# Linear attention's levels: keys and queries decayed by one product, with one exponential, and each head's scores from its own 64 partitions

## The chip, the cores and the metric

The kernel runs on one core of a Trainium2 chip. Its metric is the time of one execution on the device in microseconds, the median of several runs; lower is better.

## The reference, cut to what matters

One step of a hybrid decoder: a prompt of 2048 tokens and 64 sample tokens (8 sequences of 8) pass a norm, one input projection, two mixers, and one output projection. Mixer A is dilated window attention. Mixer B, which the change concerns, is gated linear attention (GLA) with 4 heads, key width 64 and value width 128:

```python
def step(state, xs):
    qc, kc, vc, gc = xs
    b = jnp.cumsum(gc, axis=2)
    diff = b[:, :, :, None, :] - b[:, :, None, :, :]
    decay = jnp.exp(jnp.where(causal[:, :, None], diff, -jnp.inf))
    scores = jnp.einsum('bhtk,bhsk,bhtsk->bhts', qc, kc, decay)
    o = (jnp.einsum('bhts,bhsv->bhtv', scores, vc)
         + jnp.einsum('bhtk,bhkv->bhtv', qc * jnp.exp(b), state))
    ...
```

`gc` is the log of a data-dependent forget gate. All results are float32.

## The kernel before

The program is one list of Python generators. A function `weave` interleaves the steps of several generators by their expected step counts, and that fixes the order in which instructions are written down. The framework's tile context (`schedule_with_timeline_sim=True`) then puts each engine's instructions into an order of its own, by a model of when each would be ready; every engine runs its list strictly in that order.

The stages are: projections of v, q, k with the window attention, then the projection qkb with the rest of the attention, then the GLA stage (about 820 to 1148 us of the span), then the output stage (1148 us to the end). In the GLA stage the projections g, vb and gb run on TensorE (PE) as the host work (line 1120, 24 float16 matmuls of 512 columns per tile of 128 tokens for vb and gb; g has 24 of 272 and 24 of 256), and GLA is woven between them. The weights of the output projection (w_o, two halves) are fetched and split in the same stage. The output stage combines attention and GLA per token tile (`combine`, lines 1501 to 1545), turns the result on PE (`tm`, line 1453), and multiplies by w_o (`Y`, line 1488: 48 matmuls per tile); the sample tokens' attention is woven between (values, `OS`, line 1737), and their own output `Y_s` comes near the end.

GLA for the prompt handles 256 tokens (two chunks of 128) at a time: eight groups, e0 to e7, after the 64 sample tokens. A group first turns keys, queries and gates to columns (`ptg`, `pg`, `u`), forms the running sum `b` of the log gates, and then gets the scores within a chunk in seven levels, B = 1, 2, 4, ..., 64 (the sample tokens have three). At level B the tokens are cut into pairs of blocks of B; queries of each second block meet keys of the first one, both decayed to the border between the blocks. Per level of a group (`gla_core`, lines 198 to 258):

- POOL writes `D` (lines 207 and 208): border minus `b` for first halves, `b` minus border for second halves, 128x256 each. `D` has two buffers.
- ACT takes the exponentials into `E` by three instructions (line 212): first halves for 128 partitions, and second halves apart for partitions 0 to 63 and 64 to 127, since the two heads of a pair lie on the two halves of the partitions and each gets its own slab of `E`, the other half of which stays zero.
- DVE multiplies keys by `E` into `ks` (line 219, 128x256) and queries by both slabs into `qbd` (line 223, 128x512). `E`, `ks` and `qbd` have two copies, which alternate.
- PE multiplies 64 keys with the queries of both heads at once: 8 float32 matmuls (line 247) of 128 rows, 64 keys and 2x32 queries; the zeros keep the heads apart. A float32 matmul shows as two passes, so 16 in the trace. They go to one PSUM tile of the pool `ps_S`, which has two buffers. At B = 64 there are 4 matmuls of 128 columns (line 232).
- DVE puts the scores into `Ac` where the level's mask says so (`copy_predicated`, line 253, 128x256). At B = 64, ACT copies them to `full` (line 238).

After the levels, `Ac` is copied to `full` (line 264), and for each chunk PE forms the state's update `U` (line 1280), and the output `O` (lines 1288 and 1294); `gla_out` norms it and stores it to `ob_d` (line 303). The DMAs are issued on SP's queue. Memory of the GLA stage is given back after e7's end and used again for the tiles of `combine`, the first of which is loaded as `oc` (line 1505).

Of the kernel before, what the change touches and what calls it, by code (L numbers as in the profile page):

```python
# [18 lines left out]
P = 128  # L19
D = 1024  # L20
# [32 lines left out]
def tile_hymba(ctx: ExitStack, tc: tile.TileContext, A: dict):  # L53
# [80 lines left out]
    def gla_core(pools, st, row0, n, C, levels, scan_m, mask, tagp, full=None):  # L134
# [19 lines left out]
            dd[:C].unsqueeze(2).to_broadcast([C, nch * 4, 64]),  # L154
# [4 lines left out]
        kq = gt.tile([P, 2, 2, n], F32, name=f"kq_{tagp}", tag="kqg", bufs=2)  # L159
        kT, qT = kq[:, 0], kq[:, 1]  # L160
# [37 lines left out]
        for li, B in enumerate(levels):  # L198
            bv = bf.rearrange("p (m two B) -> p m two B", two=2, B=B)
            M = 2 * n // (2 * B)  # L200
            ref = bv[:, :, 0, B - 1 : B].to_broadcast([P, M, B])


            E = st["E"][li % 2]
            D = gt.tile([P, 2, n], F32, name=f"D_{tagp}_{B}", tag="D", bufs=2)
            dv = D[:].rearrange("p a (m B) -> p a m B", B=B)
            POOL.tensor_tensor(dv[:, 1], bv[:, :, 1, :], ref, ALU.subtract)
            POOL.tensor_tensor(dv[:, 0], ref, bv[:, :, 0, :], ALU.subtract)
            for i, (rows, half) in enumerate(
                ((slice(0, P), 0), (slice(0, 64), 1), (slice(64, P), 1))  # L210
            ):
                ACT.activation(E[rows, i, :n], D[rows, half], AF.Exp, scale=1.0 / 16.0)  # L212
            ks, qbd = st["ks"][li % 2], st["qbd"][li % 2]
            kv, qv = (
                f.rearrange("p a c -> p (a c)").rearrange("p (m two B) -> p m two B", two=2, B=B)
                for f in (kT, qT)
            )
            ev = E[:, :, :n].rearrange("p i (m B) -> p i m B", B=B)
            DVE.tensor_tensor(  # L219
                ks[:, : 2 * n].rearrange("p (m two B) -> p m two B", two=2, B=B)[:, :, 0, :],  # L220
                kv[:, :, 0, :], ev[:, 0], ALU.mult,
            )
            DVE.tensor_tensor(
                qbd[:, :, :n].rearrange("p i (m B) -> p i m B", B=B),
                qv[:, :, 1, :].unsqueeze(1).to_broadcast([P, 2, M, B]), ev[:, 1:3], ALU.mult,
            )
            sc = ps_s.tile([P, 512], F32, name=f"sc_{tagp}_{B}", tag="S")
            if B == 64:

                for c in range(nch):  # L230
                    for p in range(2):
                        PE.matmul(
                            sc[:64, (c * 2 + p) * P : (c * 2 + p + 1) * P],
                            ks[:, p * n + c * C : p * n + c * C + 64],
                            qbd[:, :, (p * nch + c) * 64 : (p * nch + c + 1) * 64],
                            start=True, stop=True,
                        )
                ACT.activation(
                    full[0:64, :, 64:], sc[:64].rearrange("p (g t) -> p g t", t=64), AF.Copy
                )  # L240
                yield
                continue
            for c in range(nch):
                for p in range(2):
                    o = (c * 2 + p) * 64
                    for k0 in range(0, C, 64):
                        PE.matmul(
                            sc[k0 : k0 + 64, o : o + 64],
                            ks[:, p * n + c * C + k0 : p * n + c * C + k0 + 64],
                            qbd[:, :, p * (n // 2) + (c * C + k0) // 2 :][:, :, :32],  # L250
                            start=True, stop=True,
                        )
            DVE.copy_predicated(
                Ac[:C].rearrange("p g (m two B) -> p g m two B", two=2, B=B)[:, :, :, 1, :],
                mask[:C, li].bitcast(I32).unsqueeze(1)
                .to_broadcast([C, nch * 4, 32]).rearrange("p g (m B) -> p g m B", B=B),
                sc[:C, : nch * 128].rearrange("p (g m B) -> p g m B", g=nch * 4, B=B),
            )
            yield
# [89 lines left out]
    with ExitStack() as c1:  # L349
# [894 lines left out]
        st = {"wgu": wgu, "E": [], "ks": [], "qbd": []}  # L1244
        for i in range(2):
            for lst, nm_, shape in (
                (st["E"], "E", [P, 3, 256]), (st["ks"], "ks", [P, 512]),
                (st["qbd"], "qbd", [P, 2, 256]), (Sbd, "Sbd", [P, 2, 256]),
            ):
                t = gst.tile(shape, F32, name=f"{nm_}{i}")  # L1250
                POOL.memset(t[:], 0.0)
                lst.append(t)
# [6 lines left out]
        def gla_prompt(e):  # L1259
# [9 lines left out]
            for c in range(2):  # L1269
# [16 lines left out]
                for p in range(2):  # L1286
# [5 lines left out]
                    for j in range(2):  # L1292
                        h = 2 * p + j
                        PE.matmul(
                            O[:, h * P : (h + 1) * P], full[:, c * 4 + h, :],
# [14 lines left out]
        def sample_gla():  # L1310
# [26 lines left out]
            for p in range(2):  # L1337
# [13 lines left out]
                for j in range(2):  # L1351
                    h = 2 * p + j
                    PE.matmul(
                        O[:NS, h * P : (h + 1) * P], Am[:NS, h, :],
                        vb[:NS, h * P : (h + 1) * P], start=False, stop=(j == 1),
                    )
# [531 lines left out]
```

## Time and profile before

| | |
|---|---|
| median of 3 runs | 1423.52 us (1422.46 to 1428.86) |
| the profiled execution | 1426.68 us, of which its span 1424.9 us |
| mean granted TensorE clock | 0.966 |
| busy in the span: PE, DVE, ACT, POOL | 90%, 71%, 59%, 44% |
| GLA stage up to the last `O` (lines 1288, 1294) | to 1108.4 us |
| first `Y` matmul | 1148.2 us |

A profile line names a group of instructions by line, engine, operation and tiles, `out<-in`. PE stands for matmuls, PEld for their weight loads. In the table of windows each engine has its busy time and, in brackets, its number of instructions, and PEclk is the clock that TensorE was granted. A waits line has the total in us, the number of waits and the longest. Matmuls overlap, so a row of n matmuls lasts n pitches and one matmul's fill.

### The profile page before, as it was taken

To read this page: it belongs to the slowest core of one execution; us is meant where nothing else is said; L and a number is where in the kernel's file an instruction comes from. 1 tells how busy PE (TensorE), PEld (TensorE's weight loads), DVE (VectorE), ACT (ScalarE), POOL (GpSimd) and SP (SyncE) were. 2 spreads that over 40 slices of the span, in tenths; PEclk is the share of its full clock that TensorE was granted. 3 is DMA by queue.
4 is the path that set the end of the run, shared out by engine and by line. 5 is a ranking of instruction groups with operands and counts; after the bars stand their busy time and mean duration, and the time that the engine had idled before them with its cause. 6 is when DMAs were issued, how large, how long until landed. Compare 5 with 4: busy or idle time off the path is not lost.

```text
span 1424.9 us, 26506 instructions
## 1 busy us (share of the span) xinstructions
PE 1285.0 (90%) x8942; PEld 743.6 (52%) x8942; DVE 1018.0 (71%) x2459; ACT 843.7 (59%) x2259; POOL 621.9 (44%) x564
## 2 busy tenths in 40 slices
PE   5989999889898898996889999889999989999997
PEld 2434555455455554664667666666555434444343
DVE  6797697789798967666775357898877797773222
ACT  6466787667377775875677665777876542221120
POOL 0144355566577455554421486556551264340000
PEclk9999999999999899997999999999999999999998
DMA  8469756678966797888976444242235759998661
GB/s 297 156 188 255 192 161 150 182 203 215 240 165 173 208 288 239 260 217 228 234 190 179 149 123 116 87 153 91 88 119 176 267 179 344 359 316 267 221 215 63
DMA packets 246874, 283.27 MB, mean 199 GB/s; under 512 B 117889, under 2 KB 148690, under 8 KB 246738
## 3 DMA queue, kind: packets, MB, share of 16 engines
q1 hardware_dynamic: 246738, 281.57, 67.1%
q8 instruction: 71, 1.16, 0.4%
q14 instruction: 65, 0.53, 0.1%
HBM read 183.19 MB, written 75.24 MB: 181 GB/s over the span
## 4 chain that ended last, share of the span: by engine, by line
PE 35%; DVE 25%; DMA 16%; ACT 11%; issue 7%; POOL 4%; SPq 2%; DVEq 0%; POOLq 0%; ACTq 0%
PE Y L1488 7%; PE acc_g L1120 3%; PE acc_vb L1120 3%; PE acc_k L1120 3%; DMA k<-in_cache_k_win 2%; POOL pr L980 2%; PE s L408 2%; PE OS L1737 2%; PE acc_qkb L1120 2%; ACT p L419 2%; DMA o_d<-o 2%; DMA oc<-o_d 2%; DVE p L416 2%; PE acc_v L1120 2%; DMA T_q<-qp_d 2%
## 5 line engine op out<-in xcount | busy, mean ns | idle before, releaser
L980 POOL TENSOR_TENSOR pr<-k,qb 128x512 f32<-128x512 f32 x128 | 171.8, 1342 | 184.9 <-DVE sck L981 113.9
L1120 PEld LDWEIGHTS <-hr 128*128 128x128 f16 x1824 | 177.7, 100 | 138.2 <-issue 17.6
L419 ACT ACTIVATE p<-p,o 128x256 f32<-128x256 f32 (+1 forms) x384 | 173.1, 453 | 86.0 <-DVE o L416 83.3
L1120 PEld LDWEIGHTS <-hl 128*128 128x128 f16 x1248 | 123.2, 100 | 146.6 <-issue 22.2
L1488 PE MATMUL Y<-w_o,mh 128*128 128x512 f16 x768 | 182.9, 385 | 8.3 <-ACT mh L1454 4.9
L416 DVE CUSTOM_DVE_ANT_0 p<-s,m3w,scl_s 128x256 f32<-128x256 f32 (+1 forms) x384 | 143.6, 419 | 39.0 <-DMA o_d<-o 20.3
L393 POOL TENSOR_TENSOR pt<-p,pt 128x512 f16<-128x512 f32 (+1 forms) x80 | 98.3, 1229 | 139.6 <-ACT pt L392 107.3
L441 PE MATMUL O<-v,pt 128*128 128x128 f16 x1200 | 116.1, 224 | 25.3 <-POOL pt L393 10.0
L426 PE MATMUL t<-ident,p 128*128 128x128 f32 x600 | 119.0, 289 | 14.5 <-ACT p L419 9.2
L1488 PEld LDWEIGHTS <-mh 128*128 128x128 f16 x768 | 72.5, 99 | 103.7 <-issue 25.2
L408 PE MATMUL s<-kk,qq 128*128 128x256 f16 (+1 forms) x512 | 105.7, 326 | 17.5 <-DVE o L416 12.4
L981 DVE TENSOR_REDUCE sck<-pr 128x8 f32<-128x512 f32 x128 | 87.0, 680 | 44.0 <-POOL pr L980 43.7
L441 PEld LDWEIGHTS <-pt 128*128 128x128 f16 x1200 | 86.6, 101 | 54.6 <-POOL pt L393 13.6
L1120 PE MATMUL acc_g<-w_g,hr 128*128 128x272 f16 (+1 forms) x768 | 103.3, 285 | 1.9 <-DVE so_g L677 1.0
L1120 PE MATMUL acc_v<-w_v,hl 128*128 128x512 f16 x384 | 99.5, 405 | 4.6 <-DMA hl<-ht 3.7
L426 PEld LDWEIGHTS t<-ident,p 128*128 128x128 f32 x600 | 73.5, 146 | 43.2 <-ACT p L419 26.4
L1120 PE MATMUL acc_q<-w_q,hl 128*128 128x512 f16 x384 | 92.0, 380 | 1.9 <-ACT zs_q L703 1.4
L1120 PE MATMUL acc_k<-w_k,hl 128*128 128x512 f16 x384 | 91.3, 382 | 2.5 <-ACT w_k L658 1.3
L1454 ACT ACTIVATE mh<-tm 128x1024 f16<-128x1024 f16 x32 | 31.7, 1019 | 104.1 <-PE tm L1453 97.7
L1120 PE MATMUL acc_gb<-w_gb,hr 128*128 128x512 f16 x384 | 90.0, 388 | 2.1 <-DVE so_gb L677 2.1
L1120 PE MATMUL acc_vb<-w_vb,hr 128*128 128x512 f16 x384 | 89.3, 379 | 1.6 <-DVE so_g L677 1.6
L212 ACT ACTIVATE E<-D_e 128x256 f32<-128x256 f32 (+1 forms) x168 | 67.7, 411 | 27.1 <-DVE ks L219 17.6
(533 smaller groups left out, 2628.1 us busy)
## 6 DMA issues: line engine op xcount, KB each, us to landing
k<-in_cache_k_win SPq DMA_DIRECT2D x104, 256.0 KB, 4.3
sv<-in_cache_v_win SPq DMA_DIRECT2D x104, 256.0 KB, 5.4
hr<-h_d SPq DMA_DIRECT2D x44, 512.0 KB, 4.1
qb<-q_d SPq DMA_DIRECT2D x64, 256.0 KB, 4.6
oc<-o_d SPq DMA_DIRECT2D x48, 264.0 KB, 5.8
o_d<-o SPq DMA_DIRECT2D x64, 132.0 KB, 3.9
x<-in_x_prompt SPq DMA_DIRECT2D x16, 512.0 KB, 5.8
h_d<-hl SPq DMA_DIRECT2D x16, 512.0 KB, 4.7
```

The source lines that it names most:

```text
L212: ACT.activation(E[rows, i, :n], D[rows, half], AF.Exp, scale=1.0 / 16.0)
L393: POOL.tensor_tensor(l, f, h, ALU.subtract)
L408: PE.matmul(s_ps[:, i * w : (i + 1) * w], q, k, start=(n == 0), stop=(n == len(prods) - 1),)
L416: DVE.tensor_tensor_reduce(s[:, sl], s_ps[:, sl], mask, neg, BIG, ALU.add, ALU.min, nmf(i))
L419: ACT.activation(s[:, sl], s[:, sl], AF.Exp, bias=nmf(i), scale=-1.0, accum_out=denf(i))
L426: PE.transpose(p_ps[:, i * P : (i + 1) * P], t["s"][:, i * P : (i + 1) * P], ident[:])
L441: PE.matmul(o_, t["pt"][:, c, (i * nb + b) * P : (i * nb + b + 1) * P], vf(i, b), start=(n == 0), stop=(n == 2 * nb - 1),)
L980: POOL.tensor_tensor(pr[:], kt, qt, ALU.mult)
L981: DVE.tensor_reduce(out, pr[:].rearrange("p (u k d) -> p u k d", u=2, k=4), AX.X, ALU.add)
L1120: PE.matmul(z, a_[:, k, :], w[:, p_, k, cols], start=(k == 0 and i == 0), stop=(k == KT - 1 and i == 2),)
L1454: ACT.activation(mhl[:, a], pt[:], AF.Copy)
L1488: PE.matmul(Y[:], a_[:, k, :], w_[:, part, k, :512], start=(i == 0), stop=(i == len(prods) - 1),)
```

## The change

`E`, `ks` and `qbd` go. ACT takes the exponential of `D` in place by one instruction of 128x512. `kq`, which holds keys and then queries, becomes one row of 4n + 128 columns, so that a view of it, shifted by one block for the queries, has the first halves of the keys beside the second halves of the queries; one DVE product of 128x512 with `D` writes both into `kqd` (two copies). The heads are kept apart by their partitions: PE multiplies, for each head of a pair, 64 keys by 32 queries from partitions 0 to 63 or 64 to 127 alone. That is 16 matmuls a level in place of 8 (32 passes in place of 16), with 64 rows and 32 columns; at B = 64 it is 8 of 64 columns in place of 4 of 128. Each of the two partition halves has a PSUM tile of its own, so a level takes both buffers of `ps_S`, and there are two `copy_predicated` of 128x128 (at B = 64 two ACT copies of 64x256). The heads in `Ac` and `full` are put in another order for that.

```diff
-            E = st["E"][li % 2]
             D = gt.tile([P, 2, n], F32, name=f"D_{tagp}_{B}", tag="D", bufs=2)
...
-            for i, (rows, half) in enumerate(
-                ((slice(0, P), 0), (slice(0, 64), 1), (slice(64, P), 1))
-            ):
-                ACT.activation(E[rows, i, :n], D[rows, half], AF.Exp, scale=1.0 / 16.0)
...
+            ACT.activation(D[:], D[:], AF.Exp, scale=1.0 / 16.0)
+
+            kqd = st["kqd"][li % 2]
             DVE.tensor_tensor(
-                ks[:, : 2 * n].rearrange("p (m two B) -> p m two B", two=2, B=B)[:, :, 0, :],
-                kv[:, :, 0, :], ev[:, 0], ALU.mult,
-            )
-            DVE.tensor_tensor(
-                qbd[:, :, :n].rearrange("p i (m B) -> p i m B", B=B),
-                qv[:, :, 1, :].unsqueeze(1).to_broadcast([P, 2, M, B]), ev[:, 1:3], ALU.mult,
-            )
-            sc = ps_s.tile([P, 512], F32, name=f"sc_{tagp}_{B}", tag="S")
...
+                kqd[:, :, : 2 * n].rearrange("p a (m two B) -> p a m two B", two=2, B=B)[
+                    :, :, :, 0, :
+                ],
+                kq[:, : 2 * (2 * n + B)].rearrange("p (a x) -> p a x", a=2)[:, :, : 2 * n]
+                .rearrange("p a (m two B) -> p a m two B", two=2, B=B)[:, :, :, 0, :],
+                dv, ALU.mult,
+            )
+
+            scs = [
+                ps_s.tile([P, 512], F32, name=f"sc_{tagp}_{B}_{j}", tag="S") for j in range(2)
+            ]
             for c in range(nch):
                 for p in range(2):
-                    o = (c * 2 + p) * 64
-                    for k0 in range(0, C, 64):
-                        PE.matmul(
-                            sc[k0 : k0 + 64, o : o + 64],
-                            ks[:, p * n + c * C + k0 : p * n + c * C + k0 + 64],
-                            qbd[:, :, p * (n // 2) + (c * C + k0) // 2 :][:, :, :32],
-                            start=True, stop=True,
-                        )
-            DVE.copy_predicated(
...
+                    g = 2 * c + p
+                    for k0 in range(0, C, 64) if B < 64 else (0,):
+                        o = p * n + c * C + k0
+                        for j, sc in enumerate(scs):
+                            js = slice(64 * j, 64 * j + 64)
...
+                                PE.matmul(
+                                    sc[k0 : k0 + 64, g * 32 : g * 32 + 32],
+                                    kqd[js, 0, o : o + 64],
+                                    kqd[js, 1, o : o + 64]
+                                    .rearrange("p (m two B) -> p m two B", two=2, B=B)[:, :, 0, :],
+                                    start=True, stop=True,
+                                )
+            G = nch * 2
+            for j, sc in enumerate(scs):
+                if B == 64:
+                    ACT.activation(
+                        full[0:64, j * G : j * G + G, 64:],
+                        sc[:64, : G * 64].rearrange("p (g t) -> p g t", t=64), AF.Copy,
+                    )
+                else:
+                    DVE.copy_predicated(
+                        Ac[:C, j * G : j * G + G].rearrange("p g (m two B) -> p g m two B", two=2, B=B)[
+                            :, :, :, 1, :
+                        ],
...
```

The orders of the engines are the same up to the sample tokens' levels, and differ from there. Three places show how.

On DVE, in group e6 at levels 2 and 4 (`Ac_e` takes the scores; `rv`, `ra`, `ors` and `oss` belong to the norm of an earlier group's output, `so_gb` to the host's tile, `la` and `b` to e7's gates, `pw_o`, `wi_o` to w_o). Before:

```order
L223 TENSOR_TENSOR qbd_9616<-kq_e_12819,E_9612 128x512
L125 TENSOR_SCALAR rv_o_c_12554<-oss_c_12550 128x4
L253 COPY_PREDICATED Ac_e_12817<-gmask,sc_e_2_12879 128x128x2
L677 TENSOR_SCALAR so_gb_13763<-acc_gb_13736,wi_gb 128x512
L187 SCALAR_TENSOR_TENSOR la_e_13302<-u_e_13299,la_e_13302 128x512
L190 SCALAR_TENSOR_TENSOR b_e_13307<-scan_m,la_e_13302 128x256 x2
L129 TENSOR_TENSOR ra_o_c_12556<-rr_o_c_12555 128x4
L130 SCALAR_TENSOR_TENSOR ra_o_c_12556<-ra_o_c_12556,rv_o_c_12554 128x4
L131 SCALAR_TENSOR_TENSOR ors_c_12553<-ra_o_c_12556,rr_o_c_12555 128x4
L253 COPY_PREDICATED Ac_e_12817<-gmask,sc_e_4_12897 128x64x4
L219 TENSOR_TENSOR ks_9606<-kq_e_12819,E_9604 128x16x16
L223 TENSOR_TENSOR qbd_9608<-kq_e_12819,E_9604 128x512
```

And in the changed kernel:

```order
L254 COPY_PREDICATED Ac_e_13082<-gmask,sc_e_2_0_13148 128x64x2
L299 TENSOR_REDUCE oss_c_12916<-osq_c_12915 128x4
L254 COPY_PREDICATED Ac_e_13082<-gmask,sc_e_2_1_13149 128x64x2
L213 TENSOR_TENSOR kqd_9608<-kq_e_13084,D_e_8_13193 128x64x8
L254 COPY_PREDICATED Ac_e_13082<-gmask,sc_e_4_0_13173 128x32x4
L573 TENSOR_SCALAR pw_o_14158<-pw_o_14158 128x1
L129 TENSOR_TENSOR ra_o_c_12821<-rr_o_c_12820 128x4
L254 COPY_PREDICATED Ac_e_13082<-gmask,sc_e_4_1_13174 128x32x4
L213 TENSOR_TENSOR kqd_9604<-kq_e_13084,D_e_16_13218 128x32x16
L130 SCALAR_TENSOR_TENSOR ra_o_c_12821<-ra_o_c_12821,rv_o_c_12819 128x4
```

A level is now two copies and one product, and in e6 no `so_gb` of a host tile stands between them.

On PE, at the end of e7's last output `O` (`hr` and `acc_gb` are the host's, `ts_q` belongs to the sample tokens' attention). Before:

```order
L1120 MATMUL acc_gb_14094<-w_gb,hr_13956 128x512
L1288 MATMUL O_13557<-Sbd_9618,qe_e_13434 128x256
L1294 MATMUL O_13557<-vb_13550,full 128x128 x2
L1288 MATMUL O_13557<-Sbd_9618,qe_e_13434 128x256
L1294 MATMUL O_13557<-vb_13550,full 128x128 x2
L1120 LDWEIGHTS hr_13956
L1120 MATMUL acc_gb_14094<-w_gb,hr_13956 128x512
```

In the changed kernel:

```order
L1296 MATMUL O_13811<-vb_13804,full 128x128 x2
L1290 MATMUL O_13811<-Sbd_9606,qe_e_13789 128x256
L1296 MATMUL O_13811<-vb_13804,full 128x128 x2
L1290 MATMUL O_13912<-Sbd_9610,qe_e_13789 128x256
L1296 MATMUL O_13912<-vb_13905,full 128x128 x2
L1290 MATMUL O_13912<-Sbd_9610,qe_e_13789 128x256
L1296 MATMUL O_13912<-vb_13905,full 128x128 x2
L1639 MATMUL ts_q<-ident,ls_q 128x64 x4
```

Host matmuls that stood behind e7's last output now stand ahead of it. Counted over the whole order, of the 384 `acc_gb` matmuls of the prompt 65 stood ahead of e7's `u` (line 178) before, 188 between it and e7's last `O`, and 131 behind; now the three numbers are 286, 98 and 0. Between the `u` of one group and that of the next there are now 119 and 115 of them for the last two such stretches. Of the 98, two stand right behind e7's `u`; between them and the next stand all seven levels of e6, its update and outputs, and e7's first level.

On SP, where the first tiles of the output stage are loaded (`hr` is a reload for the host, `gw_d` its result, `oc`, `obl`, `gwl`, `gal` are loaded for `combine`). Before:

```order
L303 DMA ob_d<-ob_c_13481 128x512
L565 DMA hr_14135<-h_d 128x2048
L774 DMA gw_d<-gw_14089 128x512
L303 DMA ob_d<-ob_c_13582 128x512
L1505 DMA oc_14182<-o_d 128x528 x3
L1508 DMA obl_14187<-ob_d 128x512
L1510 DMA gwl_14189<-gw_d 128x512
L774 DMA gw_d<-gw_14130 128x512
L1512 DMA gal_14191<-ga_d 128x512
```

In the changed kernel:

```order
L306 DMA ob_d<-ob_c_13836 128x512
L1629 DMA vs_t<-v_d 64x512
L1636 DMA ls_q<-q_d 64x512
L1636 DMA ls_k<-k_d 64x512
L306 DMA ob_d<-ob_c_13937 128x512
L1655 DMA Sc_14904<-sc_d 128x2x128
L1697 DMA sm_15011<-in_c_smask 128x448
L1685 DMA k_0_14934<-in_cache_k_win 128x512
L1507 DMA oc_14537<-o_d 128x528 x3
L1510 DMA obl_14542<-ob_d 128x512
```

In both, the first `oc` comes right behind the last output of e7 (`ob_d`); host reloads and stores no longer follow it, and the sample attention's first loads now stand ahead of it.

53 lines of the change are left out of this document (20 added, 33 removed).

## The prediction

> **What bounds the kernel now.** I read the page, then the windows of the GLA stage and of the output stage, then the waits, then the groups by shape, and last the timelines of PE and SP where the two stages meet.
>
> ```profile
> span 1424.9 us, 26506 instructions
> PE 1285.0 (90%) x8942; PEld 743.6 (52%) x8942; DVE 1018.0 (71%) x2459; ACT 843.7 (59%) x2259; POOL 621.9 (44%) x564
> ```
>
> The shares are means over stages. The next rows, in windows, are one stretch each between the `u` of a group and that of the next (two rows), then from e7's `u` to the last `O`, from there to the first `Y`, and the output stage.
>
> ```profile
> 976.00:1004.60 28.60, 25.62 (x245) 18.25 (x244) 25.89 (x53) 22.24 (x58) 16.76 (x20) 1.00 0.27 86
> 1004.60:1036.60 32.00, 29.79 (x244) 18.17 (x240) 26.16 (x50) 26.08 (x67) 17.88 (x21) 1.00 0.36 106
> 1036.60:1108.40 71.80, 65.19 (x473) 37.76 (x472) 57.04 (x123) 48.22 (x118) 24.80 (x27) 0.98 0.43 137
> 1108.40:1148.20 39.80, 31.98 (x152) 14.35 (x151) 30.07 (x73) 24.44 (x52) 12.36 (x10) 0.93 0.78 270
> 1148.20:1424.90 276.70, 258.48 (x1688) 114.69 (x1688) 144.29 (x301) 57.83 (x90) 67.19 (x53) 0.97 0.73 248
> ```
>
> The columns of busy times are PE, PEld, DVE, ACT and POOL: in a group's stretch PE is busy 25.6 of 28.6 us, DVE 25.9, ACT 22.2. No engine is full; three are nearly so, and they wait for each other in turn. The waits between 820 and 1110 us say where:
>
> ```profile
> POOL D_e L207 <- ACT E L212: 62.0, 28, 7.9
> ACT E L212 <- DVE ks L219: 17.6, 15, 4.3
> PEld sc_e L247 <- issue: 15.2, 18, 2.9
> PEld sc_e L232 <- issue: 6.4, 7, 2.3
> PE sc_e L247 <- DVE qbd L223: 6.3, 7, 1.7
> PE sc_e L247 <- DVE Ac_e L253: 3.8, 4, 2.4
> PE sc_e L232 <- DVE qbd L223: 3.8, 2, 2.0
> ```
>
> The last five rows are PE's queue in front of the scores: 35.5 us, 4.4 us per group. So the stage is PE's list of matmuls plus what the chain POOL, ACT, DVE makes it wait. POOL's 62 us cost nothing by themselves.
>
> **DVE and ACT.** These groups, by shape, between 820 and 1110 us, give the prices.
>
> ```profile
> L223 DVE TENSOR_TENSOR qbd<-kq_e,E 128x512 f32<-128x512 f32 x56 | 48.1, 859 | 1.2 <-ACT E L212 1.2
> L212 ACT ACTIVATE E<-D_e 64x256 f32<-64x256 f32 x112 | 46.0, 411 | 8.7 <-DVE qbd L223 5.2 <-POOL D_e L207 2.3
> L219 DVE TENSOR_TENSOR ks<-kq_e,E 128x256 f32<-128x256 f32 x56 | 34.0, 607 | 0.0
> L247 PE MATMUL sc_e<-qbd,ks 128*64 128x64 f32 x768 | 31.7, 226 | 12.4 <-DVE qbd L223 6.3 <-DVE Ac_e L253 3.8 <-DVE pw_gb L636 1.7
> L253 DVE COPY_PREDICATED Ac_e<-gmask,sc_e 128x256 f32<-128x256 int32 x48 | 25.3, 527 | 9.3 <-PE sc_e L247 9.0
> L212 ACT ACTIVATE E<-D_e 128x256 f32<-128x256 f32 x56 | 23.0, 413 | 18.4 <-DVE ks L219 17.6 <-POOL D_e L208 0.3
> L677 DVE TENSOR_SCALAR so_gb<-acc_gb,wi_gb 128x512 f32<-128x512 f32 x10 | 7.4, 740 | 0.1
> L685 DVE CUSTOM_DVE_ANT_0 so_gb<-so_gb,sa_gb 128x512 f32<-128x512 f32 x9 | 6.6, 737 | 11.8 <-ACT sa_gb L682 11.7
> L659 DVE SCALAR_TENSOR_TENSOR w_o<-wr_o,ns_o,w_o 128x512 f16<-128x512 f32 x8 | 6.4, 836 | 0.2
> L238 ACT ACTIVATE full<-sc_e 64x512 f32<-64x512 f32 x8 | 4.6, 578 | 0.0
> L281 ACT ACTIVATE kd_e<-kd_e 128x512 f32<-128x512 f32 x8 | 5.0, 626 | 2.0 <-POOL kd_e L277 2.0
> ```
>
> DVE before: 0.86 + 0.61 + 0.53 = 2.00 us per level. After: one product of 128x512, 0.86 as `qbd`. A copy of 128x128 has no row; from 0.61 to 0.86 us for 256 more columns, 128 fewer save 0.13, so 0.40, and two are 0.80 (bounds 0.53 and 1.06). That is 1.66, so 0.34 less at 48 levels and 0.61 less at the eight of B = 64: 21 us. ACT before: 0.413 + 2 x 0.411 = 1.24 us; after 0.63 as `kd`, so 0.61 x 56 = 34 us less; two copies into `full` at 0.41 in place of one at 0.58 take 2 us back. POOL's work is unchanged. The prompt's groups thus save 2.6 us of DVE and 4 us of ACT each, on engines that are beside the path; what counts is how much PE waits less.
>
> **PE's passes.** PE's timeline has a level's scores, a level of B = 64, a burst of the sample attention that uses four strips of columns, and a run of host matmuls:
>
> ```profile
> 1088.19 0.69 PE L247 MATMUL sc_e<-qbd,ks 128*64 128x64 f32 x16 [0.51 <-DVE ra_o_c L130]
> 1091.08 1.09 PE L232 MATMUL sc_e<-qbd,ks 128*64 128x128 f32 x8
> 1175.84 0.46 PE L1671 MATMUL R<-ksT,qx 128*32 128x64 f32 x16 [0.35 <-DVE qx L1649]
> 1108.44 11.17 PE L1120 MATMUL acc_gb<-w_gb,hr 128*128 128x512 f16 x51
> ```
>
> Less one pass's 0.22 us, the scores have a pitch of 0.031 us (two 64-column strips at once), so 16 take 0.50; `R` has 0.016; the host 0.216. Now there are 32 passes of 32 columns over four quarters of the array. No row has two halves of the partitions at work at once. If they overlap fully, half of `R`'s pitch is the end below: 0.26 us; if not, 0.031 each is 0.99. I take 0.022, nearest to `R`, which also keeps four parts busy: 0.70, so 0.20 more (-0.24 to +0.49). At B = 64, 16 half passes lie between 0.50 and today's 0.94; I take 0.2 less. Over six groups (in the last two PE waits anyway, below): 36 x 0.20 - 6 x 0.2 = +6 us (-11 to +18).
>
> The Trainium skill ("TensorE: Matmul & The Clock Gate", Part 1) says that start-to-start never drops below about 25 ns; by that a level would take 0.80 us and the term would be near +10. `R`'s 16 ns speaks against it as a floor between different tiles of the array.
>
> **The order.** Counted in the new order, 221 more `acc_gb` matmuls stand ahead of e7's `u`. A full group's stretch holds 115 to 119 of them, 25 us, beside some 10 us of its own, where DVE needs about 26 us (26.2, less 2.6, and 1.75 host tiles more at 1.48 = 2.6). DVE falls from 82 to 91% of the stretch to some 73%. Of the first six groups' 27 us of waits I leave a third: -18 us (-27 to 0).
>
> The price comes behind. e6 now has no host work between its levels, and a level takes both buffers of `ps_S`, so PE to DVE to PE runs in turn. From e7's `u` to the last `O` DVE has 57.0 us, less 2 x 2.6, less 90/24 host tiles at 1.48 (5.6), and 8 x 0.84 for the second half of w_o, which now falls here: 53 us. At the same share, 57.0 of 71.8, the stretch is 67 us. Before it would have been 71.8 - 90 x 0.216 = 52.4 without the 90 matmuls that moved, and their host time is only moved; 2 to 3 us are passes. So +12 us (+4 to +21).
>
> Then the seam. Before, after the last `O`, PE had this to do, and SP issued the first tile of `combine`:
>
> ```profile
> L1120 PE MATMUL acc_gb<-w_gb,hr 128*128 128x512 f16 x131 | 30.6, 394 | 2.1 <-DVE so_gb L677 2.1
> ...
> 1118.18 0.32 SPq L303 DMA_DIRECT2D ob_d<-ob_c  x1
> 1118.55 1.39 SPq L1505 DMA_DIRECT2D oc<-o_d  x3
> ...
> 1148.24 7.73 PE L1488 MATMUL Y<-w_o,mh 128*128 128x512 f16 x24 [4.86 <-ACT mh L1454]
> ```
>
> 131 x 0.216 = 28.3 of the 39.8 us were host work, 11.5 were not. Now nothing is left to cover the way from `O` over its norm, `ob_d`, `oc`, `combine`, `tm` and `mh` to `Y`. It took 9.8 us to SP and 29.7 from there, with DVE and ACT shared with host tiles and w_o. That work is gone, so 39.5 is the upper end; the lower is 19, the 5.8 us in which `oc` lands with some 13 us of its operations, taken as an estimate from how DVE, POOL and ACT are spaced there. I take 24: +12 us (+8 to +28).
>
> Last, the end of the output stage: the sample's last norm waits for a round over memory.
>
> ```profile
> 1402.51 0.69 PE L1465 MATMUL mt_s<-ident,mix_s 64*128 64x64 f32 x4 [4.11 <-DVE mix_s L1566]
> 1404.13 6.03 PE L1488 MATMUL Y_s<-w_o,mh_s 128*128 128x512 f16 x16 [0.94 <-DVE mh_s L1471]
> ```
>
> The new order has the sample attention earlier against `Y`, and 48 `Y` matmuls (10.4 us) between its last `OS` and this `mt_s`, so these 5 us go, with some 3 us of matmuls and waits that move ahead of `Y`: -8 us (-12 to 0).
>
> The sum: +6 - 18 + 12 + 12 - 8 = +4 us on the profiled execution's own 1426.68 (span 1424.9 and 1.8 around it). The median of the runs stands 3.2 us below that, so 1423.5 + 4 = 1428 us, rounded up.
>
> **The rivals.** *Faster:* the halves of the partitions overlap and the relief is whole. Passes 0, waits -27, the last two groups +6, seam +9, end -8: -20 us, 1403. For it: 55 us less on two engines that were 80 to 90% busy, and one step less from `D` to the scores. Against it: the order has moved the host work to where it no longer covers. The Trainium skill ("TensorEngine Tiling (Array Packing)", Tiling Modes) says that tiles run LdWeights and Matmul in parallel, which is this rival's condition; no row here shows it for halves of the partitions.
>
> *Slower:* with both PSUM buffers in one level, PE's next scores wait for both copies. A turn is 0.70 + 0.22 + 0.80 and one other DVE instruction, 0.74: 2.5 us. Where host matmuls between two levels fill less than that, it decides; in e6 they fill nothing. If e6 and e7 take 77 us in place of 67 and the first six keep half of their waits (-13), with passes at +11: +24 us, 1447. For it: `PE sc_e <- DVE Ac_e`, 3.8 us, was there with two buffers for two levels. Against it: in the first six groups 3 to 4 us of host work lie between levels. The Trainium skill's same page (Restrictions and Gotchas) warns that row tiling raises PSUM pressure, since different row tiles go to different banks; that is this rival's cause.
>
> *Absorbed:* the output stage is set by loads (DMA 0.73 of its time, 248 GB/s), and a later first `Y` with earlier sample loads ends at the same time: within 2 us of before, 1424.
>
> **How the numbers follow.** What a measurement of this kernel can tell from no change is about 0.5%, 7 us. My forecast, 1428 (its own range 1420 to 1431), has 0.28, the absorbed case 0.10, so 0.38 within 0.5%; the slower rival 0.35, the faster 0.27. The range takes both in with their bounds: 1402 to 1450.
>
> **What would show it.** Right: `kqd` near 0.86 us and 2 copies near 0.40; scores of a level over 0.7 to 0.9 us; DVE near 75% in a group's stretch; PE idle in e6, and about 24 us without host work ahead of the first `Y`; no wait at `mt_s`. Wrong: score passes at 0.016 or less; groups ending as early as before, with PE's waits gone; or `Y` beginning well past 1165 us, if the PSUM turn rules all groups.

## The result, and the profile after

| | before | changed |
|---|---|---|
| median | 1423.67 us of 4 (1422.46 to 1428.86) | 1450.47 us of 4 (1445.35 to 1454.29) |
| profiled execution | 1426.68 us | 1450.24 us |

The ratio is 1.0178 (95% interval 1.0158 to 1.0197): slower by 25 us. The median stands at the upper end of the stated range, 1450, half a microsecond past it, and not at the forecast, 1428: it is near the time that the prediction had given to its slower rival, 1447. The page of the changed kernel has all engines but PE less busy than before:

```profile
span 1448.5 us, 28093 instructions
PE 1302.9 (90%) x9786; PEld 754.2 (52%) x9786; DVE 986.1 (68%) x2451; ACT 813.7 (56%) x2149; POOL 615.8 (43%) x560
```

Its windows, in the order of the prediction's: the last two stretches from one `u` to the next, then from e7's `u` to the last `O`, to the first `Y`, and the output stage (busy times of PE, PEld, DVE, ACT, POOL, then the granted clock, the DMA share and GB/s):

```profile
996.60:1038.70 42.10, 39.86 (x387) 22.08 (x385) 26.05 (x58) 25.40 (x59) 21.75 (x25) 0.96 0.36 120
1038.70:1080.50 41.80, 39.45 (x385) 22.23 (x381) 23.12 (x49) 17.66 (x41) 17.29 (x21) 0.96 0.32 106
1080.50:1153.40 72.90, 60.44 (x638) 40.89 (x634) 56.52 (x134) 51.51 (x117) 30.18 (x32) 0.79 0.28 93
1153.40:1180.30 26.90, 6.90 (x52) 4.86 (x53) 18.80 (x54) 6.79 (x17) 11.29 (x10) 0.59 0.87 299
1180.30:1448.50 268.20, 255.67 (x1655) 111.53 (x1652) 135.49 (x285) 55.12 (x85) 58.89 (x47) 0.98 0.74 253
```

A group's stretch is 42 us in place of 29 to 32, with the host work that moved into it; DVE is busy in only 55 to 62% of it, and the clock, 1.00 before, is 0.96; from e7's `u` to the last `O` it is 0.79 (0.98 before). The groups by shape, between 820 and 1110 us, give the new prices:

```profile
L213 DVE TENSOR_TENSOR kqd<-kq_e,D_e 128x512 f32<-128x512 f32 x50 | 40.2, 803 | 16.4 <-PE sc_e L234 9.4 <-PE sc_e L239 5.3 <-ACT D_e L210 1.7
L239 PE MATMUL sc_e<-kqd 64*64 64x32 f32 x1344 | 36.6, 228 | 4.0 <-DVE Ac_e L254 3.8
L210 ACT ACTIVATE D_e<-D_e 128x512 f32<-128x512 f32 x51 | 32.0, 631 | 35.6 <-POOL D_e L209 31.4 <-DVE Sbd L1303 3.8
L254 DVE COPY_PREDICATED Ac_e<-gmask,sc_e 128x128 f32<-128x128 int32 x84 | 24.9, 347 | 34.4 <-PE sc_e L239 34.1
```

So a level takes DVE 0.80 + 2 x 0.35 = 1.50 us (2.00 before) and ACT 0.63 (1.24). The saving is there, and more of it than forecast. The waits of the stage, 815 to 1154 us, show that PE gains little by it:

```profile
PEld sc_e L239 <- issue: 8.0, 23, 0.4
PE ptk_e L290 <- ACT ob_c L305: 6.5, 3, 2.2
PEld sc_e L239 <- DVE Ac_e L254: 5.8, 8, 1.8
PE sc_e L239 <- DVE Ac_e L254: 3.8, 4, 1.6
```

The waits in front of the scores are fewer, but others have come (`ptk_e`, 1.7 us before), and `Ac_e` is now the first cause where the scores do wait. PE's timeline has two levels of e4, with host matmuls between them, and its level of B = 64, and then e6's levels, with no host work between them:

```profile
1027.22 0.67 PE L239 MATMUL sc_e<-kqd 64*64 64x32 f32 x32
1027.82 5.14 PE L1123 MATMUL acc_gb<-w_gb,hr 128*128 128x512 f16 x23
1032.89 0.67 PE L239 MATMUL sc_e<-kqd 64*64 64x32 f32 x32
...
1038.12 0.68 PE L234 MATMUL sc_e<-kqd 64*64 64x64 f32 x16
...
1088.97 3.72 PE L239 MATMUL sc_e<-kqd 64*64 64x32 f32 x64 [1.64 <-DVE Ac_e L254]
...
1098.98 1.08 PE L239 MATMUL sc_e<-kqd 64*64 64x32 f32 x32
...
1106.62 1.12 PE L234 MATMUL sc_e<-kqd 64*64 64x64 f32 x16 [2.77 <-DVE ra_o_c L130]
```

Less 0.22 us for the last one, the 31 passes before it take 0.45 us, 14.5 ns each: the halves of the partitions do overlap. In e6 the same 32 passes take 1.08 us. The windows of that piece say why:

```profile
1087.00:1097.00 10.00, 6.86 (x114) 5.91 (x108) 9.04 (x24) 4.92 (x16) 8.33 (x9) 0.65 0.16 54
1097.00:1111.00 14.00, 5.89 (x68) 4.03 (x68) 12.26 (x25) 13.17 (x32) 5.63 (x7) 0.50 0.56 169
1111.00:1120.00 9.00, 9.00 (x68) 7.66 (x70) 6.12 (x16) 7.81 (x20) 5.42 (x7) 0.50 0.24 89
1120.00:1147.00 27.00, 27.00 (x272) 13.92 (x270) 21.60 (x54) 17.95 (x38) 7.15 (x8) 0.99 0.18 62
```

PE had waited, and its granted clock went to half. The Trainium skill ("TensorE: Matmul & The Clock Gate", Part 1) says that the clock halves after an idle window of some 3.4 us and comes back after a busy one; the trace agrees as far as its 0.50 goes. The longest wait ahead of the fall is 1.64 us, though, and from 1111 to 1120 us PE shows as busy without a gap while its clock stays at 0.50; it is back at 0.99 where host matmuls stand between the levels again. Then the way to the first `Y`, and the sample's last norm:

```profile
1177.75 1.04 PE L1455 MATMUL tm<-ident,mt 128*128 128x128 f16 x8 [10.02 <-ACT mt L1445]
...
1180.35 1.89 PE L1490 MATMUL Y<-w_o,mh 128*128 128x512 f16 x4
...
1425.34 0.46 PE L1467 MATMUL mt_s<-ident,mix_s 64*128 64x64 f32 x4
```

### The profile page after: what moved, and what is told of

It reads as the page before. It is cut to its first block, busy times and chain, and to the rows that moved or that the text cites. A ratio compares the mean times of both kernels' runs of the same rounds, so it can differ in the third digit from the quotient of the medians.

```text
span 1448.5 us, 28093 instructions
## 1 busy us (share of the span) xinstructions
PE 1302.9 (90%) x9786; PEld 754.2 (52%) x9786; DVE 986.1 (68%) x2451; ACT 813.7 (56%) x2149; POOL 615.8 (43%) x560
## 5 line engine op out<-in xcount | busy, mean ns | idle before, releaser
L1123 PEld LDWEIGHTS <-hr 128*128 128x128 f16 x1824 | 177.7, 100 | 132.1 <-issue 12.7
L208 POOL TENSOR_TENSOR D_e<-b_e 128x256 f32<-128x256 f32 x56 | 38.3, 684 | 102.5 <-DVE kqd L213 82.0
```

What stands on the lines that cost most here:

```text
L1123: PE.matmul(z, a_[:, k, :], w[:, p_, k, cols], start=(k == 0 and i == 0), stop=(k == KT - 1 and i == 2),)
```

## The experiments

For each run two windows count: from e0's `u` to the last `O`, and from there to the end (the tail). Host matmuls that the order moves between the two change both, so I take 0.216 us for each `acc_gb` out of its window; what is left I call bare. The stretch ahead of e0's `u` isn't used: with the same order it took 822.0 us in the profile before and 815.6 in the one after, and over all the runs it lies between 814.0 and 823.1. A few us between two single profiles thus say little. Before and changed kernel:

```profile
822.00:1108.60 286.60, 264.75 (x2181) 171.00 (x2181) 228.27 (x468) 204.39 (x521) 158.14 (x178) 0.98 0.38 117
1108.60:1424.90 316.30, 290.25 (x1839) 128.91 (x1836) 174.16 (x373) 82.27 (x141) 79.55 (x62) 0.96 0.74 251
```

```profile
815.60:1153.40 337.80, 312.61 (x3158) 196.53 (x3157) 215.18 (x493) 195.15 (x451) 160.69 (x181) 0.92 0.35 110
1153.40:1448.50 295.10, 262.58 (x1704) 116.40 (x1704) 154.29 (x338) 61.91 (x102) 70.17 (x56) 0.95 0.75 257
```

Before: 286.6 less 253 x 0.216 is 232.0 bare, and 316.3 less 131 x 0.216 is 288.0. Changed: 337.8 less 384 x 0.216 is 254.9, and 295.1. So 23 us are lost in the GLA stage and 7 in the tail. PE was idle for 25.2 us of the stage, and for 21.9 before (the length less the busy time), so 3 of the 23 are waiting. The other 20 are busy time of PE beside the moved host matmuls: 229.7 us against 210.1. The lower clock can account for that: if all of a stage's time goes with it, a mean of 0.92 costs 337.8 x 0.08 = 27 us, and 0.98 before cost 286.6 x 0.02 = 6, an estimate from these rows.

My two theories at the start: *placement* (the host work has left the places that need it) and *turn* (a level that takes both `ps_S` buffers is slower in itself). The first runs hold the host work of one kernel where the other has it, by order alone (for the first of them the step counts given to `weave` are changed as well).

**The changed kernel with the host work placed as before.**

```diff
+    GATES = {("gb", 3): ("u", "e7"), ..., ("gb", 11): ("O", 15), ...}
...
+    if after is not None and k == i == 0:
+        hold.enter_context(tc.issue_after(MARK[after].ins))
     PE.matmul(z, a_[:, k, :], w[:, p_, k, cols], ...
```

> The changed kernel, with the host matmuls (g, vb, gb) held on PE, by order alone and without a wait, behind the same groups as before the change: 72 of acc_gb ahead of e7's u, 192 from there to the last O, 120 behind it (before: 65, 188, 131; changed: 286, 98, 0). Placement theory (the loss comes from the host work having left e6, e7 and the way from the last O to the first Y; those two stretches gave 20.5 and 15.4 us more idle PE than before): 1412 to 1428 us, the clock back at 1.0 in e6, the first Y at most 12 us behind the last O's host work. Turn theory (a level that takes both buffers of ps_S is slower wherever the host work stands): 1438 to 1455 us, the idle time of PE moves into the first six groups, in front of sc_e.

1.0118 (1.0087 to 1.0149), 1444.0 us. Placement falls as the whole cause: it gives back 9 us. (The expectation's 20.5 and 15.4 us are what the two stretches got longer without the moved host work; PE's idle time in them rose by 5.9 and 12.2.)

```profile
818.10:1136.30 318.20, 292.98 (x3039) 187.67 (x3039) 201.23 (x473) 185.63 (x434) 155.02 (x179) 0.92 0.36 111
1136.30:1441.50 305.20, 284.81 (x1825) 128.06 (x1822) 163.56 (x358) 72.02 (x120) 73.90 (x60) 0.96 0.76 254
```

Bare, 261.2 and 279.3 us: the tail is mended, the stage is worse still.

**The kernel before with the host work placed as in the changed one.**

```diff
+    PULL = {"e2": ("g1", 11), ..., "e7": ("gb", 11)}
...
+    hold.enter_context(tc.issue_after(HOST[ahead_].ins))
     PE.matmul(u[:, p * n : (p + 1) * n], ...
```

> The kernel before, with the u of e2 to e7 held on PE, by order alone, behind as much host work as in the changed kernel: 288 acc_gb ahead of e7's u, 96 behind it, none behind the last O. DVE, ACT and the scores are as before. Placement theory: 1443 to 1458 us, with the clock near 0.5 to 0.6 between the last O and the first Y. Turn theory: at most 1430 us, since a level takes one buffer of two here and e6 runs through its levels faster than the 20 us that the changed kernel lost there.

1.0031 (1.0015 to 1.0046), 1430.45 us: 4 us. The bare way from the last `O` to `Y` was there too, with its clock at 0.62 (33.3 us), but the tail as a whole was shorter than before:

```profile
823.00:1148.20 325.20, 297.88 (x2314) 184.81 (x2313) 252.82 (x506) 224.87 (x560) 175.58 (x188) 0.97 0.36 114
1148.20:1431.50 283.30, 259.58 (x1705) 116.31 (x1704) 149.21 (x336) 62.09 (x102) 63.78 (x52) 0.95 0.79 267
```

The stage is 242.3 us bare, +10, the tail -5: what the gap costs, the output stage gives back.

**The second half's scores in another pool.**

```diff
-    ps_s.tile([P, 512], F32, name=f"sc_{tagp}_{B}_{j}", tag="S") for j in range(2)
+    pool.tile([P, 512], F32, name=f"sc_{tagp}_{B}_{j}", tag=tag)
+    for j, (pool, tag) in enumerate(((ps_s, "S"), (ps_t, "O")))
```

> The changed kernel with the second half's scores in a tile of ps_O in place of a second one of ps_S, so that two levels can be in PSUM at once, as before the change. By its order 226 acc_gb stand ahead of e7's u, 158 from there to the last O, none behind it. Turn theory: 1420 to 1432 us, PE's waits in front of sc_e for Ac_e gone. Placement theory: between the two kernels, 1434 to 1446 us: e6 and e7 have 60 matmuls more beside them than in the changed kernel, but the way to the first Y is as bare as there (13 to 18 us of idle PE).

0.9993 (0.9976 to 1.0009), 1425.96 us: as fast as before, as the turn theory had it. But its rows show that the reason was mostly another:

```profile
816.80:1150.60 333.80, 314.83 (x3174) 201.06 (x3173) 216.88 (x500) 195.62 (x456) 167.98 (x188) 0.94 0.39 122
1150.60:1429.80 279.20, 256.37 (x1688) 114.47 (x1688) 149.60 (x330) 60.06 (x99) 64.24 (x51) 0.96 0.76 258
```

The stage is 250.9 us bare, 4 less than in the changed kernel; the tail is 16 less. The profiled execution took 1431.6 us, 6 more than the median.

**One exponential and one product, scores as before.**

```diff
-    scs = [ps_s.tile(...) for j in range(2)]
+    sc = ps_s.tile([P, 512], F32, name=f"sc_{tagp}_{B}", tag="S")
...
+    PE.matmul(sc[k0 : k0 + 64, g * 2 * w : (g + 1) * 2 * w], kqd[:, 0, o : o + 64],
+        kqd[:, 1, o : o + 64]...unsqueeze(1).to_broadcast([P, 2, ...]), start=True, stop=True)
```

> The changed kernel's one exponential and one product, with the scores' shape of before: eight matmuls a level over all 128 partitions with 64 columns (the two heads of a pair are summed, so the scores differ from the reference's), one PSUM tile, one copy_predicated of 128x256. By its order no acc_gb stands ahead of e7's u, 151 from there to the last O, 233 behind it. Relief theory (DVE's and ACT's saved work, 0.9 and 0.6 us a level, shortens the groups): 1395 to 1412 us. If PE's list bounds the stage and its waits do not go with that work: 1418 to 1428 us. Both the placement and the turn theory put it at or below the kernel before.

0.9822 (0.9797 to 0.9848), 1401.6 us. The relief is real, 25 us, where the scores keep their shape, though the scheduler's order is another one here too (0, 151 and 233 `acc_gb` in place of 65, 188 and 131). The clock stays at 1.00:

```profile
818.70:1067.40 248.70, 236.39 (x2080) 158.84 (x2079) 196.50 (x394) 161.20 (x385) 152.64 (x172) 1.00 0.39 120
1067.40:1399.70 332.30, 310.43 (x1941) 137.35 (x1938) 178.06 (x385) 90.65 (x162) 85.04 (x66) 0.98 0.74 250
```

Bare, 216.1 and 282.0 us. The next runs add the rest of the change to this one.

**Two copies out of one tile.**

```diff
-    DVE.copy_predicated(Ac[:C]..., sc[:C, : G * 32]...)
+    for j in range(2):
+        DVE.copy_predicated(Ac[:C, j * G : j * G + G]..., sc[:C, j * G * 32 : (j + 1) * G * 32]...)
```

> The run with one product and the scores' shape of before (1401.6 us), with two copy_predicated of 128x128 per level in place of one of 128x256, out of the same one ps_S tile. The heads of a pair are summed, so the scores differ from the reference's. By its order the host work stands as in that run (152 acc_gb between e7's u and the last O, 232 behind; 151 and 233 there). If the second ps_S tile is what cost 37 us between that run and the one with two banks (1438.7 us): 1400 to 1408 us. If it was the second copy on DVE: 1425 to 1440 us.

0.9849 (0.9830 to 0.9868), 1404.1 us. The second copy costs 2 to 4 us.

**The host work pulled ahead as the second tile makes it** (the edit of the second run, on the one-product kernel).

> The run with one product and the scores' shape of before (1401.6 us; heads of a pair summed), one ps_S tile and one copy, but with the u of e2 to e7 held on PE, by order alone, behind as much host work as stands there in the run with two banks (1438.7 us): 288 acc_gb ahead of e7's u, 96 behind, none behind the last O. If placement carries the loss of the second tile: 1428 to 1442 us. If the levels' turn over two tiles costs it directly, and placement as little as with the kernel before (+4 us): 1402 to 1412 us.

0.9943 (0.9925 to 0.9960), 1418.58 us: neither number. Placement costs 17 us here, nearly half of what the second tile brings. Bare, 314.1 less 384 x 0.216 is 231.2 us (+15), the tail -1; the profiled execution took 1413.4 us, 5 less than the median:

```profile
816.10:1130.20 314.10, 294.69 (x2314) 184.88 (x2313) 222.58 (x444) 190.59 (x443) 172.40 (x186) 0.97 0.38 119
1130.20:1411.30 281.10, 255.58 (x1704) 116.34 (x1704) 150.78 (x335) 62.12 (x102) 65.10 (x52) 0.95 0.80 269
```

**Two `ps_S` tiles a level, matmuls over all partitions.**

```diff
-    sc = ps_s.tile([P, 512], F32, name=f"sc_{tagp}_{B}", tag="S")
+    scs = [ps_s.tile([P, 512], F32, name=f"sc_{tagp}_{B}_{p}", tag="S") for p in range(2)]
```

> As the run with one product and the scores' shape of before (1401.6 us), but the scores of each pair of heads go to a ps_S tile of their own and two copy_predicated of 128x128 take them, as in the changed kernel. The matmuls are the same eight over all 128 partitions; the heads of a pair are again summed, so the scores differ from the reference's. By its order 287 acc_gb stand ahead of e7's u, 97 from there to the last O, none behind it. Turn theory (the second ps_S tile per level is what costs): 1438 to 1458 us, the whole way up to the changed kernel. Row theory (the matmuls on half of the partitions cost, in time on PE or in what the scheduler takes them for): 1398 to 1412 us.

1.0093 (1.0068 to 1.0118), 1438.7 us: 37 above the one-tile run, 35 above it with two copies. The second tile is what costs, but for the last 12 us up to the changed kernel; whether by a turn over the buffers, the rows have to say.

```profile
823.10:1144.50 321.40, 299.44 (x2314) 185.93 (x2313) 214.58 (x492) 194.68 (x449) 160.32 (x183) 0.96 0.37 115
1144.50:1438.90 294.40, 261.59 (x1704) 116.18 (x1704) 149.33 (x339) 62.01 (x104) 67.46 (x56) 0.94 0.76 258
```

Bare, 238.5 us, 7 more than with placement alone; the tail has 13 more. What differs in the tail is when the sample attention begins. Its first `OS` on `P3x`, in the run before this one, in this one and in the changed kernel (start of the first and of the last):

```profile
L1736 PE MATMUL OS<-sv,P3x x256: 379/379/403, 1163.8 to 1376.2; 128*32 128x256 f32 x128
```

```profile
L1731 PE MATMUL OS<-sv,P3x x256: 379/391/403, 1203.6 to 1399.8; 128*32 128x256 f32 x128
```

```profile
L1739 PE MATMUL OS<-sv,P3x x256: 378/380/404, 1215.8 to 1409.4; 128*32 128x256 f32 x128
```

That is 34, 59 and 62 us behind the last `O`. The two slow tails don't use the gap ahead of `Y` for it. The other three runs with no host work behind the last `O` fit: where it begins 31 to 35 us behind (the second and the third run) the tail is 283.3 and 279.2 us, where it begins 66 us behind (the scores part alone, next) 293.4. Why the order has it so late there isn't shown.

**The scores part alone**, on the kernel before (E, `ks`, `qbd` and three exponentials kept).

```diff
-    sc = ps_s.tile([P, 512], F32, name=f"sc_{tagp}_{B}", tag="S")
+    scs = [ps_s.tile([P, 512], F32, name=f"sc_{tagp}_{B}_{j}", tag="S") for j in range(2)]
...
+    PE.matmul(sc[k0 : k0 + 64, g * w : g * w + w], ks[js, o : o + 64],
+        qbd[js, j, p * (n // 2) + (c * C + k0) // 2 :][:, :w], start=True, stop=True)
```

> The kernel before with the scores part of the change alone: E, ks and qbd, three exponentials and two products as before, but the scores of each half of the partitions in a ps_S tile of its own, by 16 matmuls of 32 columns, and two copies. By its order 288 acc_gb ahead of e7's u, 96 behind, none behind the last O. If the two parts of the change add up (one product gave -25 us alone, the whole +23): 1468 to 1482 us. If the turn over PSUM bounds a level whatever DVE and ACT save, so that their relief is lost behind it: 1446 to 1460 us, near the changed kernel.

1.0227 (1.0199 to 1.0254), 1457.4 us. The parts don't add up: behind the new scores the product is worth 7 us (1457 to 1450), not 25.

```profile
818.10:1163.40 345.30, 312.37 (x3158) 196.41 (x3157) 241.28 (x552) 228.70 (x568) 162.00 (x184) 0.93 0.34 107
```

**Both at once: host work held, second half in the other pool** (the edits of the first and the third run).

> The run with the host work held as before the change (1444 us), but the second half's scores in a tile of ps_O, so that two levels fit in PSUM. Placement is the same as in that run to within 4 matmuls a group. Turn theory: 1412 to 1426 us, the idle time in the first six groups down from 56 to at most 42 us. If the rest of the scores part (two copies, 32 passes) is what costs: 1436 to 1448 us.

1.0142 (1.0107 to 1.0177), 1445.92 us. My turn theory misses by 20 us. With the host work held, room for two levels brought nothing: the scores waited less for `Ac_e` (the first row is of the held run, the others of this one) and more for the product, and the stage stayed long (254.7 us bare, 311.7 less 264 x 0.216):

```profile
PE sc_e L242 <- DVE Ac_e L257: 5.6, 4, 2.1
PE sc_e L243 <- DVE kqd L216: 7.4, 7, 2.4
PE sc_e L243 <- DVE Ac_e L258: 3.3, 1, 3.3
```

**One exponential, the queries' halves on DVE and POOL.**

```diff
+    ACT.activation(D[:], D[:], AF.Exp, scale=1.0 / 16.0)
...
+    for j, eng in enumerate((DVE, POOL)):
+        eng.tensor_tensor(qbd[js, j, :n]..., qv[js, :, 1, :], dv[js, 1], ALU.mult)
```

> A version of the change that keeps one PSUM tile, eight full matmuls and one copy per level: one exponential of 128x512 in place; DVE multiplies the keys (128x256) and the first head's queries (64x256) into ks and qbd, POOL the second head's queries (64x256). ACT saves 0.61 us a level, DVE about 0.26 (0.86 less 0.60), POOL gets about 0.69 more. By its order 16 acc_gb ahead of e7's u, 185 from there to the last O, 183 behind. If relief of ACT and DVE with one ps_S tile is what shortens the groups: 1404 to 1418 us, faster than before. If POOL's part of the chain eats it: 1422 to 1432 us.

1.0069 (1.0045 to 1.0093), 1435.25 us: slower than either expectation. The stage is 245.0 us bare (288.4 less 201 x 0.216), with POOL busy for 199 us of it in place of 158. That POOL's link in the chain costs more than ACT and DVE save would fit, but isn't shown: the clock is lower as well, 0.94.

```profile
821.70:1110.10 288.40, 262.45 (x2130) 171.54 (x2130) 231.44 (x464) 168.92 (x398) 198.96 (x234) 0.94 0.36 111
```

**Both heads in one tile, rows and columns of the array on the diagonal.**

```diff
+    sc = ps_s.tile([P, 512], F32, name=f"sc_{tagp}_{B}", tag="S")
...
+    PE.matmul(sc[js, g * 32 : g * 32 + 32], kqd[js, 0, o : o + 64], kqd[js, 1, o : o + 64]...)
...
+    DVE.tensor_copy(d2[64 * j : 64 * j + 64, :, k], dd[64 * k : 64 * k + 64]...)
```

> The changed kernel's one exponential, one product and 16 matmuls on half of the partitions, but the prompt's head j of a pair also takes columns 64j to 64j+63 of the array, so that both heads' scores lie in one ps_S tile, on the two halves of its partitions, with one copy_predicated of 128x256 per level (at the end of a group Ac goes to full by four ACT copies of 64x256). All outputs are computed. By its order no acc_gb stands ahead of e7's u, 98 from there to the last O, 286 behind. Turn theory: 1394 to 1412 us, about the run with one product, 15 to 30 us faster than before. If matmuls on half of the partitions cost by themselves (the 11.8 us between the two-bank run and the changed kernel): 1408 to 1424 us.

1.0120 (1.0097 to 1.0143), 1442.85 us: both expectations miss. But the run doesn't show what half matmuls cost in the changed kernel, since this version has costs of its own. Rows and columns go in pairs, so two quarters of the array are at work and not four, and the passes take twice as long: 2.05 us less 0.22, over 63, is 29 ns each at a clock of 1.00. There are also four small copies of the diagonal per group:

```profile
1076.54 2.05 PE L253 MATMUL sc_e<-kqd 64*64 64x32 f32 x64
1076.50:1078.60 2.10, 2.10 (x67) 2.02 (x68) 2.10 (x5) 1.55 (x4) 2.10 (x3) 1.00 0.00 0
L155 DVE COPY d_e<-dd_e 64x4 f32<-64x4 f32 x30 | 14.0, 466 | 0.4
```

A level takes PE 0.93 us in place of 0.50: 48 x 0.43 less 8 x 0.41 at B = 64 (0.68 us in place of 1.09) is 17 us more than in the one-product run. The bare stage exceeds that run's by 43 us (280.5 less 98 x 0.216 is 259.3, against 216.1). Of these, 37 are busy time of PE, which the passes and the clock (0.07 of 280.5 us, 20 by the estimate above) account for; 6 are waits, the copies' part among them.

```profile
818.80:1099.30 280.50, 261.82 (x2868) 183.81 (x2868) 197.44 (x410) 161.71 (x397) 149.82 (x169) 0.93 0.32 96
```

**The same, with host work placed about as before** (the edit of the second run on it).

> The run with one PSUM tile for both heads (the diagonal, 1442.9 us; all outputs computed), with the u of e2 to e7 held on PE, by order alone, behind about as much host work as before the change: 72, 72, 96, 72, 72 host matmuls in the stretches from e2's u to e7's u (43, 50, 59, 41, 127 there; 81, 75, 89, 79, 65 before), 146 from e7's u to the last O, 166 behind. Cover theory (with little host work between them, levels leave PE idle, the granted clock falls to half, and that slows the levels again; 41 us of the diagonal's GLA stage ran at half clock): 1396 to 1416 us, at most 10 us at half clock between e0's u and the last O. Row theory (matmuls on half of the partitions let the clock fall, whatever stands between them; every kernel with them had 41 us or more at half clock there, those without at most 34): 1428 to 1445 us, with 20 us or more at half clock.

1.0130 (1.0109 to 1.0151), 1445.27 us. That is the row theory's end of the two: cover does not mend it, and the clock stays low, 0.94 (37 us at half clock, if it is only ever whole or half, an estimate). The passes are the diagonal's here too, so it is no proof for the changed kernel's:

```profile
814.00:1120.10 306.10, 285.72 (x2990) 193.95 (x2990) 211.70 (x439) 175.86 (x426) 154.66 (x174) 0.94 0.36 108
```

## Why the prediction was off where it was

**What made the kernel slower.** The one-product run, and what is put on it step by step, to the changed kernel:

| step | ratio to before | bare GLA stage | bare tail |
|---|---|---|---|
| before | 1 | 232.0 | 288.0 |
| one exponential, one product | 0.9822 | 216.1 | 282.0 |
| + host work pulled ahead | 0.9943 | 231.2 | 281.1 |
| + second `ps_S` tile, second copy | 1.0093 | 238.5 | 294.4 |
| + matmuls on half of the partitions | 1.0178 | 254.9 | 295.1 |

So the first half of the change is worth 25 us, and the scores take 50 back in three ways: the order that the scheduler makes of them (17 us), the second tile and copy beside that (21; the profiles have 13 of it in the tail and 7 in the stage), and the half matmuls (12). That the order comes from the second tile is shown by the count: with two copies and one tile no `acc_gb` stands ahead of e7's `u`, with two tiles 287. The shares depend on the sequence of the steps, since the parts don't add up. The three rows in the middle sum the two heads of a pair: they are experiments, no versions of the kernel.

**Point by point**, at 0.216 us for each moved host matmul:

- *DVE and ACT*: right, and more was saved (1.50 us of DVE per level, forecast 1.66; ACT 0.63 as forecast).
- *Passes*, +6 forecast: wrong sign. A level's row is 0.67 us against 0.69 before, and one of B = 64 is 0.68 against 1.09: 36 x 0.02 and 6 x 0.41 less, about -3 us. By the 25 ns of the Trainium skill's "TensorE: Matmul & The Clock Gate", Part 1, a level's 32 passes would have taken 0.80 us; the 14.5 ns measured, 0.46 us, decide against it.
- *Waits of the first six groups*, -18 forecast: this is the step that failed. The stretch from e0's `u` to e7's is 264.9 us against 214.6, with 221 x 0.216 = 47.7 of host work more in it: +2.6 where passes and waits together were put at -12.

```profile
822.00:1036.60 214.60, 199.36 (x1709) 133.11 (x1708) 171.03 (x345) 156.18 (x404) 133.34 (x151) 0.98 0.37 110
815.60:1080.50 264.90, 252.17 (x2524) 155.64 (x2523) 158.66 (x359) 143.64 (x334) 130.50 (x149) 0.96 0.37 114
```

  "Of the first six groups' 27 us of waits I leave a third" counted weight loads that waited while matmuls still ran: PE itself was idle for only 15.2 us there (214.6 less 199.4), less than the 18 that were to go. Its waits in front of the scores did go, from 10.0 to 0.8 us, but others came (`ptk_e` 8.5, 1.7 before; `O_s` 2.8), so 12.7 us are left. And PE's busy time grew by 5 us more than the host work, at a clock of 0.96 in place of 0.98, for which the prediction had no term. With one tile the same relief took 16 us off the bare stage.
- *e6 and e7*, +12 forecast: +20.5 (72.9 against 52.4), near the upper bound. Of it 5.9 us are idle time of PE (12.5 against 6.6). The rest is PE busy for longer at a clock of 0.79, for which neither the forecast nor the rival had a term. The rival's picture, PE behind `Ac_e` with both buffers taken, is there but small: 2.9 us of PE's waits in this stretch, 2.4 before.
- *The seam*, +12 forecast: +15.4 (26.9 against 11.5). *The end*, -8: -8.5, and no wait at `mt_s`.

The sum of these is +30, of which 6.4 us of the unexplained start come off to the +23.6 of the profiled executions. The slower rival had the result's sign and size, in part by luck. In the table's sequence its second tile is the larger part of the cause, 38 of the 50 us, but 17 of them come by the order and 13 lie in the tail; 7 are in the stage, where a turn over two buffers would show, and with the host work held a second pool brought nothing. It had no part for the half matmuls or the clock.

**What stays open.** Why the half matmuls cost, when PE spends less on them. All seven kernels that have them take 250.9 to 262.4 us bare in the GLA stage, at a mean clock of 0.92 to 0.94; the seven without take 216.1 to 245.0 at 0.94 to 1.00. In the table's last step the bare stage grows by 16 us: PE's busy time beside the host work by 13 (229.7 against 216.5), its idle time by 3. The clock, 0.92 in place of 0.96, gives 14 by the estimate above. So most of what they cost there is the clock, but whether they let it fall, or the order made around 16 matmuls in place of 8 does, no run separates. Nor did I find a version that computes all outputs and beats both kernels.

## What to carry to other kernels

A change that splits one result over two tiles of a pool with two buffers leaves none for the next step: count the buffers per step before counting what the engines save, and then run it, for here a second pool gave the time back with the scheduler's own order and nothing with the host work held. Where a scheduler sets the order, such a step also moves unrelated work, so run the halves of a change apart: here the same relief gave 25 us behind the old scores and 7 behind the new ones. Before asking what PE waits for, see whether it is idle for longer at all: in this stage it was mostly busy at a lower clock.

## What the runs showed of the hardware

Matmuls on the two halves of the partitions overlap: 32 float32 passes of 32 columns over four quarters of the array take 14.5 ns each, and over two quarters on the diagonal 29 ns. A stretch in which PE mostly waits pays twice: at the clock of 0.50 the same 32 passes took 1.08 us in place of 0.67. The clock fell behind a wait of 1.64 us and stayed at 0.50 through 9 us in which PE showed as busy without a gap. Of the 32 copies of 64x4 float32 on DVE half took at most 0.17 us and the longest 1.86; their mean, 0.47, is that of a few long ones.
